# Attention and conformer kernel on one core: the sink logit as a column of the softmax, an early output projection taken apart, and a first stage in another order

## The chip, the cores and the metric

One core of one Trainium2 chip runs the whole kernel. The metric is device time in microseconds of one execution; the time before is 1807.06 us, the median of three runs (1806.05, 1807.06, 1809.84). One more execution was profiled: it took 1802.25 us.

## The reference, cut to what matters

Two layers on a stream of 1024 latent tokens of width 1024, with 256 context tokens. Layer 0 is windowed attention: 16 query heads of width 128, 4 key/value heads, a window of 128 tokens to each side, the 256 context keys in the same softmax, and one learned sink logit per head. Layer 1 is a conformer convolution module. The parts that the change touches:

```python
def sink_softmax(sink_l, *parts):
    sink_col = jnp.broadcast_to(sink_l..., first.shape[:-1] + (1,))
    p = jax.nn.softmax(jnp.concatenate([sink_col, *parts], axis=-1), axis=-1)
    ...                      # the sink's own column is dropped

for i in range(DEPTH):
    shift, scale, gate = jnp.split((silu_c @ ada_w[i] + ada_b[i])[:, None, :], 3, axis=-1)
    h_lat = modulate(rmsnorm(x, norm_g[i]), shift, scale)
    ...
    # attention: q, k, v, z = h_lat @ w_in; rope on q, k; y = (o * silu(z)) @ w_out
    x = x + gate * y
return rmsnorm(x, final_g)
```

So the sink takes part in the row's maximum and in the row's sum, and gives no output of its own.

## The kernel before, in words

Every large product is computed as three: each float32 operand is split into a high part (a copy rounded to the matmul's input type, `hi`) and a low part (`lo = full - hi`), and TensorE adds hi·hi, hi·lo and lo·hi. So each weight chunk and each activation tile costs a copy (mostly on ScalarE, ACT) and a subtraction (`split_lo`, on VectorE, DVE, or GpSimd, POOL) before TensorE (PE) may use it. In the profile these are `whi`/`wlo` for input weights (128x1024), `hh`/`hl` for the normalised tokens, `ahi`/`alo` for the modulation weights, `woh`/`wol` for the output weights, `ozh`/`ozl` for the gated attention output, `pthi`/`ptlo` for the transposed probabilities, `qh`/`ql`, `kh`/`kl`, `vh`/`vl` for queries, keys and values.

**First stage (0 to about 130 us).** Four row tiles `xs0` of 128 tokens are loaded, their sums of squares go to `sums`, `rstd_of` makes the factor `r` of a row in seven small operations on 128x4 elements (ACT's square root `sq`, DVE's `rr`, three `rq` and `r`), `normalise` scales the rows (two on DVE, two on ACT), PE turns them (`turn`, transposes by `ident`), `x_tile` applies the modulation and splits, `x_mm` multiplies by the chunks of k, q, v of head group 0. Before PE can do that, chunk 0 of the weights is split by `wsA.split(G)`: both halves on POOL. Then the second half of the tokens (`xs1`) follows in the same way, with `normalise(xs1, ...)` in the loop over `pr`. The rotary position of k and q (`finish`, lines 811 to 834) is a chain of a multiplication by `cos` (DVE), one by `sin` (POOL), a sum (DVE), a copy (ACT, `kh`/`qh`) and a subtraction (POOL, `kl`/`ql`); its last three steps are put off as one closure, `last`, in a deque `ropes0`, and one is popped per pass of the loop over `kt` at lines 1044 to 1060.

**Attention (130 to 860 us).** 16 heads times 8 query blocks. For each block `scores` (line 934) issues six matmuls into PSUM, a DVE reduction that adds the mask, writes `p` and gives the row maximum `mx`; a 128x1 operation on DVE that turns `mx` and the sink into `nmx` = min(-SCALE·mx, -sink); an exponential of the block on ACT with `nmx` as bias and the row sum `l0` as by-product; a second exponential of the sink alone, 128x1 (`es`); a 128x1 sum `l0 + es` and a reciprocal `ri` on DVE; and POOL scales `p` by `ri`. `fill(12)` then gives PE twelve matmuls of the next head's projections, `transposes` turns the scaled `p`, ACT copies the result (`pthi`) and DVE takes the difference (`ptlo`), and `pv` multiplies by v after every fourth block. In the background DVE builds the modulation of layer 1 (`mask_page`, scalar_tensor_tensor), takes low parts of the output weights (`low_parts`, `low_page`; a scheduling edge `after(..., anchor_max)` puts each behind the `nmx` of the last block), ACT makes `whi` and POOL `wlo` of the next weight chunk.

**Output projection of the attention (`proj_attn`, lines 645 to 735).** A generator. For each row pair `i` it loads `wo`, `wol` and (for the first column half) `ozf` (SyncE's queue, SP), splits them (`woh`, `ozh` on ACT, `ozl` on DVE) and multiplies. `EARLY_ROWS = 6` rows of it run in head 15 as filler matmuls: at step (15, 4) (line 1085, `EARLY_FROM = 4`) all of `lows` is run out and `EA + 1 = 3` steps of `projA` are taken. From 905 us on the rest of it, the conv layer and its output follow.

**What sets the order.** PE's order is the program's throughout. In the first stage DVE and ACT (`pin("PVA")`, later `pin("PV")`) are in program order too; from the attention on a list scheduler sets the order of ACT, DVE, POOL and SP at build time, and each engine then works its list strictly in order. So an instruction that waits holds back all that stands behind it on its engine. Tiles live in a pool of 45 pages (`pg`); `p` of a block and `wraw` of a weight chunk are such pages, so a first write to a page can also wait for the last reader of what lay in it before. In the trace all helper calls have line 88; so groups are told apart by tile names.

Of the kernel before, what the change touches and what calls it, by code (L numbers as in the profile page):

```python
# [12 lines left out]
ALU = mybir.AluOpType  # L13

P = 128
# [78 lines left out]
def backbone_kernel(  # L94
# [105 lines left out]
    class WStream:  # L200
# [19 lines left out]
        def split(self, hi_eng=None):  # L220
# [53 lines left out]
    wsA = WStream(chunks, nraw=4, lo_eng=lambda i: V if i in (2, 3) else G)  # L274
# [66 lines left out]
    def normalise(ts, ss, engs):  # L341
        r = rstd_of(ss, D, len(ts))
        for i, eng in enumerate(engs):
            if eng is A:
                act(ts[i], ts[i], AF.Copy, scale=r[:, i:i + 1])
            else:
                eng.tensor_scalar(out=ts[i], in0=ts[i], scalar1=r[:, i:i + 1], scalar2=1.0, op0=ALU.mult, op1=ALU.mult)

# [127 lines left out]
    normalise(xs0, ss0, (V, V, A, A))  # L476
    wsA.split(G)
# [13 lines left out]
    for pr in range(NPR):  # L491
# [4 lines left out]
        if pr + 2 < NPR:  # L496
            ada_split(pr + 2, (0, 1))
        x_mm(a, 0, acc0, which)
# [11 lines left out]
        if pr == 2:  # L510
            normalise(xs1, ss1, (G, G, A, G))
# [124 lines left out]
    def proj_attn():  # L636
# [64 lines left out]
        for i, (s, kk) in enumerate(seqB):  # L701
# [112 lines left out]
    def rope(o, sl, dh, dl, ropes=None):  # L814
# [16 lines left out]
        if ropes is None:  # L831
            last()
        else:
            ropes.append(last)
# [99 lines left out]
    def scores(h, qb):  # L934
# [14 lines left out]
        sc8 = small([P, 5], name="sc", bufs=6)  # L949
        mx, nmx, l0, es, ri = (sc8[:, i:i + 1] for i in range(5))  # L950
        w = nw + CT
        sc = dict(scale=1.0, scalar=-3.0e38, op0=ALU.add, op1=ALU.max, accum_out=mx)
        if qb == TB - 1:
            V.tensor_tensor_reduce(
# [4 lines left out]
        else:  # L959
            V.tensor_tensor_reduce(out=p[:, 0:w], in0=s[:, w0:768], in1=mask[:, 640 - w:640], **sc)  # L960
# [82 lines left out]
    for kt in range(KT):  # L1043
# [3 lines left out]
        if kt > 0 and ropes0:  # L1047
            ropes0.popleft()()
# [640 lines left out]
```

## Time and profile before

| | |
|---|---|
| runs shown | 1806.05, 1807.06, 1809.84 us; median 1807.06 |
| profiled execution | 1802.25 us; its span from first to last instruction 1800.5 us |
| mean granted TensorE clock | 0.988 |
| PE busy | 1725.7 us |
| DVE, ACT, POOL busy | 1247.2, 890.2, 787.9 us |
| instructions in the trace | 24003 |

The views are read as follows. A row of a timeline has start, duration, engine, operation and output <- inputs; in square brackets the idle time of the engine before it and what ended it. A row of the waits names the waiting engine and tile, who released it, the total, the count and the longest. A row of the windows has the length of a stretch, the busy time of each engine in it (count), the granted clock of TensorE as a share of full speed (PEclk), the DMA engines' busy share and GB/s. In the trace the DVE reduction of a block is CUSTOM_DVE_ANT_0 (or ANT_1) with a DVE_READ_ACCUMULATOR2_ANT behind it; in the order below both are "ISA".

### The profile page before, as it was taken

How to read it: one execution, taken by the hardware profiler on the slowest of the kernel's cores; microseconds unless marked ns; L12 is line 12 of the kernel's file. 1: busy time of each engine (PE TensorE's matmuls, PEld its weight loads, DVE VectorE, ACT ScalarE, POOL GpSimd, SP SyncE). 2: the span in 40 equal slices, each digit the busy share in tenths (PEclk: the TensorE clock that was granted, in tenths of full speed). 3: DMA queues.
4: the chain of work that ended last, by engine and by line, in shares of the span. 5: the costliest groups of instructions: out<-in, count | busy, mean ns of one | idle time of the engine just before them, and what ended most of it. 6: DMA issues, size and time to landing. Idle time of an engine off the chain costs nothing. (4 is left out here: it accounts for less than half of the span.)

```text
span 1800.5 us, 24003 instructions
## 1 busy us (share of the span) xinstructions
PE 1725.7 (96%) x8383; PEld 1419.1 (79%) x8383; DVE 1247.2 (69%) x2418; ACT 890.2 (49%) x1539; POOL 787.9 (44%) x614
## 2 busy tenths in 40 slices
PE   5989999999999999999899999999999999999997
PEld 2678888888887888788688887888888888788886
DVE  6766774776656774676513349999999999866823
ACT  6645553445434454444423436655656565366730
POOL 1243443333423344333100137998988789120300
PEclk8999999999999999999899999999999999999999
DMA  9224443444324443335676633111020202376981
GB/s 316 92 71 126 132 135 91 131 131 142 110 94 129 146 136 105 110 97 177 250 269 234 237 119 106 47 36 48 24 88 30 82 31 72 115 240 236 327 279 47
DMA packets 195327, 242.47 MB, mean 135 GB/s; under 512 B 11799, under 2 KB 126791, under 8 KB 195205
## 3 DMA queue, kind: packets, MB, share of 16 engines
q1 hardware_dynamic: 188516, 230.10, 38.8%
q10 hardware_dynamic: 6688, 10.83, 2.6%
q8 instruction: 66, 1.08, 0.2%
q14 instruction: 57, 0.46, 0.1%
HBM read 188.70 MB, written 41.69 MB: 128 GB/s over the span
## 5 line engine op out<-in xcount | busy, mean ns | idle before, releaser
L88 POOL TENSOR_TENSOR odd_half<-odd_half,prod_half 128x513 f32<-128x513 f32 (+2 forms) x252 | 318.1, 1269 | 21.0 <-ACT prod_half L88 7.5
L88 PE MATMUL psg<-hh_page,whi_page 128*128 128x512 f32 x600 | 238.3, 397 | 0.0
L88 PE MATMUL psg<-hh_page,wlo_page 128*128 128x512 f32 x600 | 237.3, 395 | 0.0
L88 PE MATMUL psg<-hl_page,whi_page 128*128 128x512 f32 x600 | 237.1, 395 | 0.0
L88 POOL TENSOR_SCALAR p_page<-p_page,sc 128x640 f32<-128x640 f32 (+1 forms) x128 | 104.5, 816 | 302.7 <-DVE sc L88 153.7
L88 POOL TENSOR_TENSOR wlo_page<-wraw_page,whi_page 128x1024 fp32r<-128x1024 f32 x72 | 175.3, 2436 | 122.6 <-ACT whi_page L88 88.9
L88 ACT ACTIVATE prod_half<-ubuf,dww 128x513 f32<-128x513 f32 (+2 forms) x252 | 165.0, 674 | 110.2 <-POOL odd_half L88 105.9
L88 PE MATMUL psg<-h2l_page,whi_page 128*128 128x512 f32 x456 | 179.3, 393 | 1.8 <-DVE h2l_page L88 1.8
L88 PE MATMUL psg<-h2h_page,whi_page 128*128 128x512 f32 x456 | 180.5, 396 | 0.0
L88 PE MATMUL psg<-h2h_page,wlo_page 128*128 128x512 f32 x456 | 179.5, 394 | 0.0
L88 ACT ACTIVATE p_page<-p_page,sc 128x640 f32<-128x640 f32 (+1 forms) x128 | 102.5, 801 | 142.7 <-DVE sc L88 135.6
L88 DVE SCALAR_TENSOR_TENSOR pss<-ubuf,wsum,pss 128x512 f32<-128x512 f32 (+3 forms) x270 | 172.6, 673 | 0.3
L88 DVE SCALAR_TENSOR_TENSOR pss<-ubuf,dww,pss 128x512 f32<-128x512 f32 (+3 forms) x270 | 172.4, 673 | 0.3
L88 PEld LDWEIGHTS psg<-hh_page,wlo_page 128*128 128x128 f32 x600 | 113.2, 189 | 26.6
L88 DVE TENSOR_TENSOR ptlo<-pss,pthi 128x640 fp32r<-128x640 f32 (+1 forms) x144 | 103.0, 716 | 41.8 <-ACT pthi L88 41.2
L88 PEld LDWEIGHTS psg<-hl_page,whi_page 128*128 128x128 f32 x600 | 113.4, 189 | 20.5
L88 PEld LDWEIGHTS psg<-hh_page,whi_page 128*128 128x128 f32 x600 | 113.3, 189 | 20.3
L88 ACT ACTIVATE pthi<-pss 128x640 fp32r<-128x640 f32 (+1 forms) x144 | 88.1, 612 | 83.1 <-PE pss L88 75.8
L88 ACT ACTIVATE whi_page<-wraw_page 128x1024 fp32r<-128x1024 f32 x87 | 91.6, 1054 | 69.1 <-PE psg L88 22.0
L88 PE MATMUL pso<-h2h_page,whi_page 128*128 128x512 f32 x312 | 122.9, 394 | 0.0
L88 PE MATMUL pso<-h2l_page,whi_page 128*128 128x512 f32 x312 | 122.8, 394 | 0.0
L88 PE MATMUL pso<-h2h_page,wlo_page 128*128 128x512 f32 x312 | 122.7, 393 | 0.0
(243 smaller groups left out, 4098.3 us busy)
## 6 DMA issues: line engine op xcount, KB each, us to landing
wraw_page<-in_conv_w_in_dram SPq DMA_DIRECT2D x48, 512.0 KB
wraw_page<-in_attn_w_in_dram SPq DMA_DIRECT2D x40, 512.0 KB
wo_page<-in_attn_w_out_dram SPq DMA_DIRECT2D x32, 512.0 KB
wol_page<-wolA SPq DMA_DIRECT2D x32, 512.0 KB
wo_page<-in_conv_w_out_dram SPq DMA_DIRECT2D x32, 512.0 KB
wol_page<-wolC SPq DMA_DIRECT2D x32, 512.0 KB
rope_half<-rope_half ACTq DMA_DIRECT2D x80, 128.0 KB
araw_page<-in_ada_w_dram SPq DMA_DIRECT2D x32, 256.0 KB
```

The lines of the kernel that those rows point to most:

```text
L88: r = f(*a, **k)
```

## The change

**Softmax.** `mx` and `es` go. The reduction multiplies by -SCALE itself, starts from the negative sink (`scalar=nsink`, a column of 128 values) and takes the minimum, so that its accumulator is `nmx`. ACT copies the negative sink into one more column `w` of `p` (128x1, from a constant), and one exponential over `w + 1` columns (641 or 513 in place of 640 or 512) gives `p` and the row sum with the sink in it. Per block, and there are 128, two 128x1 DVE operations and one 128x1 exponential go, one 128x1 copy on ACT comes. `low_parts` are now behind the reduction itself.

**Early output projection.** `run(lows)` and the first step of `projA` move from step (15, 4) to (15, 2), and one step each is taken at (15, 2), (15, 3), (15, 4). The last early row no longer splits the row after it. The loads of the residual rows `xr` are issued at `kk == 4` in place of 3.

**First stage.** The row factors `r` are computed before chunk 0 is split; its high part goes from POOL to ACT, its low part from POOL to DVE, and the scaling of the rows stands between the two. `normalise(xs1)` stands before `x_mm(a)` of `pr == 2` in place of behind it. The closure `last` becomes two, `add` and `low`; `low` is on DVE instead of POOL there, and pops begin at `kt > 2`.

```diff
-                if hi_eng:
-                    hi_eng.tensor_copy(h, r)
-                else:
-                    act(h, r, AF.Copy)
+                act(h, r, AF.Copy)
+                if between:
+                    between()
                 split_lo(self.lo_eng(i), l, r, h)
...
-    wsA = WStream(chunks, nraw=4, lo_eng=lambda i: V if i in (2, 3) else G)
+    wsA = WStream(chunks, nraw=4, lo_eng=lambda i: V if i in (0, 2, 3) else G)
...
-    normalise(xs0, ss0, (V, V, A, A))
-    wsA.split(G)
+    r0 = rstd_of(ss0, D, 4)
+    wsA.split(lambda: scale_rows(xs0, r0, (V, V, A, A)))
...
+        if pr == 2:
+            normalise(xs1, ss1, (G, G, A, G))
         x_mm(a, 0, acc0, which)
...
-            ahead(i, EA, 1)
+            ahead(i, EA, min(1, EARLY_ROWS - 1 - i))
...
-            if kk == 3:
+            if kk == 4:
...
-        def last():
+        def add():
             tt(V, r, r, w, ALU.add)
             act(dh, r, AF.Copy)
-            split_lo(G, dl, r, dh)
+
+        def low():
+            split_lo(G if ropes is None else V, dl, r, dh)
...
-        mx, nmx, l0, es, ri = (sc8[:, i:i + 1] for i in range(5))
+        nmx, l0, ri = (sc8[:, i:i + 1] for i in range(3))
         w = nw + CT
-        sc = dict(scale=1.0, scalar=-3.0e38, op0=ALU.add, op1=ALU.max, accum_out=mx)
+
+        act(p[:, w:w + 1], nsink[:, h:h + 1], AF.Copy)
+        sc = dict(scale=-SCALE, scalar=nsink[:, h:h + 1], op0=ALU.add, op1=ALU.min, accum_out=nmx)
...
-        anchor_max[:] = [V.tensor_scalar(out=nmx, in0=mx, scalar1=-SCALE, scalar2=nsink[:, h:h + 1], op0=ALU.mult, op1=ALU.min)]
-        act(p[:, 0:w], p[:, 0:w], AF.Exp, bias=nmx, scale=SCALE, accum_out=l0)
-        act(es, sink[:, h:h + 1], AF.Exp, bias=nmx)
-        tt(V, l0, l0, es, ALU.add)
+        anchor_max[:] = [least]
+        act(p[:, 0:w + 1], p[:, 0:w + 1], AF.Exp, bias=nmx, scale=-1.0, accum_out=l0)
         V.reciprocal(ri, l0)
...
-        if kt > 0 and ropes0:
+        if kt > 2 and ropes0:
             ropes0.popleft()()
...
+        if (h, qb) == (NH - 1, EARLY_FROM - 2):
+            run(lows)
+        if h == NH - 1 and EARLY_FROM - 2 <= qb < EARLY_FROM:
+            next(projA)
         if (h, qb) == (NH - 1, EARLY_FROM):
-            run(lows)
-            for _ in range(EA + 1):
-                next(projA)
+            next(projA)
             fillq.append((("wo", 0), early_proj()))
```

Three places show what stands where afterwards. The first is DVE's list in the first stage, from the last steps of the row factors (`rq`, `r`) to the first tiles of normalised tokens (`hf`, `hl`), before:

```order
L88 TENSOR_SCALAR rq_9_241<-rq_9_241 128x4
L88 TENSOR_TENSOR r_10_245<-rr_8_239,rq_9_241 128x4
L88 TENSOR_SCALAR x_page_97<-x_page_97,r_10_245 128x1024
L88 TENSOR_SCALAR x_page_98<-x_page_98,r_10_245 128x1024
L88 TENSOR_SCALAR hf_page_277<-psg_263,mod_176 128x512
L88 TENSOR_TENSOR hl_page_276<-hf_page_277,hh_page_275 128x512
```

and after:

```order
L88 TENSOR_SCALAR rq_9_241<-rq_9_241 128x4
L88 TENSOR_TENSOR r_10_245<-rr_8_239,rq_9_241 128x4
L88 TENSOR_SCALAR x_page_97<-x_page_97,r_10_245 128x1024
L88 TENSOR_SCALAR x_page_98<-x_page_98,r_10_245 128x1024
L88 TENSOR_TENSOR wlo_page_248<-wraw_page_105,whi_page_247 128x1024
L88 TENSOR_SCALAR hf_page_277<-psg_263,mod_176 128x512
L88 TENSOR_TENSOR hl_page_276<-hf_page_277,hh_page_275 128x512
```

One row has come, chunk 0's low part, behind the scaling; POOL's list loses both rows of chunk 0, and ACT's gets the high part ahead of its two rows `x_page`.

The second is DVE's list at the step from the last block of head 12 to the first of head 13: `sc_7062` is the small tile of the block (13, 0), the reductions are "ISA", and `rope_half` belongs to q of head 13. Before:

```order
L88 ISA p_page_7061,sc_7062<-pss_7054,mask_page_699 128x512
L88 ISA sc_7062 128x1
L88 TENSOR_TENSOR rope_half_7078<-psg_6962,cos_page_623 128x512
L88 TENSOR_TENSOR ptlo<-pss_7042,pthi 128x5x128
L88 SCALAR_TENSOR_TENSOR mask_page_699<-dww_raw,cs,mask_page_699 128x256
L88 TENSOR_SCALAR sc_7062<-sc_7062,nsink 128x1
L88 TENSOR_TENSOR low_page_7052<-low_page_7052,lhi_half_7110 128x512
L88 TENSOR_TENSOR sc_7062<-sc_7062 128x1
L88 RECIPROCAL sc_7062<-sc_7062 128x1
L88 TENSOR_TENSOR ptlo<-pss_7100,pthi 128x5x128
L88 SCALAR_TENSOR_TENSOR mask_page_699<-wsum_raw,cs,mask_page_699 128x256
L88 TENSOR_TENSOR rope_half_7078<-rope_half_7078,rope_half_7077 128x512
```

The same place after, where the small tile is `sc_6856` and the rope is `rope_half_6870`:

```order
L88 TENSOR_TENSOR rope_half_6870<-psg_6758,cos_page_623 128x512
L88 ISA p_page_6855,sc_6856<-pss_6848,mask_page_699,nsink 128x512
L88 ISA sc_6856 128x1
L88 TENSOR_TENSOR low_page_6846<-low_page_6846,lhi_half_6902 128x512
L88 TENSOR_TENSOR ptlo<-pss_6836,pthi 128x5x128
L88 SCALAR_TENSOR_TENSOR mask_page_699<-dww_raw,cs,mask_page_699 128x256
L88 RECIPROCAL sc_6856<-sc_6856 128x1
L88 TENSOR_TENSOR ptlo<-pss_6892,pthi 128x5x128
L88 SCALAR_TENSOR_TENSOR mask_page_699<-wsum_raw,cs,mask_page_699 128x256
L88 TENSOR_TENSOR rope_half_6870<-rope_half_6870,rope_half_6869 128x512
```

The small operation between the reduction and the exponential is gone, and with it the four rows that stood ahead of it; the low part has moved ahead of the first `ptlo`.

The third is ACT's list at the end of the last head, where `pthi` are copies of the last blocks' transposes and `woh`, `ozh` the splits of the output projection. Before:

```order
L88 ACTIVATE woh_page_8401<-wo_page_8364 128x1024
L88 ACTIVATE p_page_8275,sc_8276<-p_page_8275,sc_8276 128x640
L88 ACTIVATE sc_8276<-sink,sc_8276 128x1
L88 ACTIVATE pthi<-pss_8308 128x5x128
L88 ACTIVATE p_page_8323,sc_8324<-p_page_8323,sc_8324 128x512
L88 ACTIVATE sc_8324<-sink,sc_8324 128x1
L88 ACTIVATE woh_page_8622<-wo_page_8444 128x1024
L88 ACTIVATE pthi<-pss_8356 128x5x128
L88 ACTIVATE woh_page_8450<-wo_page_8395 128x1024
L88 ACTIVATE pthi<-pss_8388 128x4x128
L88 ACTIVATE ozh_page_8624<-ozf_page_8448 128x1024
```

After:

```order
L88 ACTIVATE p_page_8023,sc_8024<-p_page_8023,sc_8024 128x641
L88 ACTIVATE pthi<-pss_8054 128x5x128
L88 ACTIVATE woh_page_8332<-wo_page_8139 128x1024
L88 ACTIVATE ozh_page_8334<-ozf_page_8143 128x1024
L88 ACTIVATE p_page_8069,sc_8070<-p_page_8069,sc_8070 128x513
L88 ACTIVATE pthi<-pss_8100 128x5x128
L88 ACTIVATE pthi<-pss_8132 128x4x128
L88 ACTIVATE woh_page_8366<-wo_page_8188 128x1024
L88 ACTIVATE ozh_page_8368<-ozf_page_8192 128x1024
```

The two splits of output weights that stood ahead of the last two `pthi` are behind them or further ahead; none stands between the last exponential and the last `pthi`.

More of the change, by code (lines that the diff above doesn't have):

```diff
@@ L218, in load, with split @@
             self.nl += 1
-        def split(self, hi_eng=None):
+        def split(self, between=None):
             if self.ns >= self.nl:
@@ L339, in sums, with scale_rows @@
         return ss
-    def normalise(ts, ss, engs):
-        r = rstd_of(ss, D, len(ts))
+    def scale_rows(ts, r, engs):
         for i, eng in enumerate(engs):
@@ L347, in normalise @@
                 eng.tensor_scalar(out=ts[i], in0=ts[i], scalar1=r[:, i:i + 1], scalar2=1.0, op0=ALU.mult, op1=ALU.mult)
+    def normalise(ts, ss, engs):
+        scale_rows(ts, rstd_of(ss, D, len(ts)), engs)
     mods = [ctile([P, 4, 2], F32, f"mod{pr}") for pr in range(NPR)]
@@ L509, in backbone_kernel @@
             ssc = sums(cx, (A, A))
-        if pr == 2:
-            normalise(xs1, ss1, (G, G, A, G))
         if pr > 1:
@@ L831, in rope @@
         if ropes is None:
-            last()
+            add()
+            low()
         else:
-            ropes.append(last)
+            ropes.extend((add, low))
     vlate = {}
@@ L948, in scores @@
         p = pg.alloc(F32, [1024], "p")
-        sc8 = small([P, 5], name="sc", bufs=6)
-        mx, nmx, l0, es, ri = (sc8[:, i:i + 1] for i in range(5))
+        sc8 = small([P, 3], name="sc", bufs=6)
+        nmx, l0, ri = (sc8[:, i:i + 1] for i in range(3))
         w = nw + CT
-        sc = dict(scale=1.0, scalar=-3.0e38, op0=ALU.add, op1=ALU.max, accum_out=mx)
+        act(p[:, w:w + 1], nsink[:, h:h + 1], AF.Copy)
+        sc = dict(scale=-SCALE, scalar=nsink[:, h:h + 1], op0=ALU.add, op1=ALU.min, accum_out=nmx)
         if qb == TB - 1:
-            V.tensor_tensor_reduce(
+            least = V.tensor_tensor_reduce(
                 out=p[:, 0:w].rearrange("p (a b) -> p a b", a=2),
```

2 lines of the change are left out of this document (1 added, 1 removed).

## The prediction

> **What bounds the kernel now.** I read the page's busy times first, then the windows by stage, then the waits of TensorE (PE), then the timelines at its longest waits. The page:
>
> ```profile
> PE 1725.7 (96%) x8383; PEld 1419.1 (79%) x8383; DVE 1247.2 (69%) x2418; ACT 890.2 (49%) x1539; POOL 787.9 (44%) x614
> ```
>
> PE's matmuls are the same before and after, so all that can be won lies in the time in which PE stands, and in the stretches in which it works at a lower clock. The windows say in which stages those lie:
>
> ```profile
> 0.00:42.00 42.00, 21.92 (x74) 9.47 (x74) 25.80 (x36) 27.21 (x33) 6.98 (x10) 0.80 0.97 310
> 42.00:130.00 88.00, 77.48 (x410) 59.22 (x410) 61.02 (x109) 46.30 (x82) 30.48 (x22) 1.00 0.31 95
> 130.00:860.00 730.00, 706.21 (x3857) 602.14 (x3855) 483.02 (x1113) 342.57 (x724) 275.17 (x226) 1.00 0.41 125
> 860.00:905.00 45.00, 37.62 (x177) 31.91 (x177) 20.41 (x39) 19.46 (x31) 6.42 (x16) 0.89 0.67 242
> 905.00:1790.00 885.00, 882.25 (x3872) 716.40 (x3870) 651.20 (x1106) 453.57 (x669) 468.88 (x340) 1.00 0.40 132
> ```
>
> The second figure is PE's busy time. It stands 20.1 us up to 42, 10.5 to 130, 23.8 in the attention, 7.4 at its end, and 2.8 in the 885 us after it, 64.6 in all. That last row carries the argument: behind 905 us PE is the bound without a gap, so what is won ahead of it arrives at the end in full. The waits name who releases PE:
>
> ```profile
> PE pss L88 <- POOL p_page L88: 9.4, 14, 2.2
> PE psg L88 <- DVE x_page L88: 7.2, 2, 7.0
> PE pso L88 <- ACT pthi L88: 5.9, 3, 4.2
> PE pss L88 <- DVE sc L88: 5.8, 5, 3.2
> PE pso L88 <- DVE ptlo L88: 4.4, 6, 1.8
> PE psg L88 <- POOL x_page L88: 1.7, 2, 0.9
> ```
>
> The first, third and fourth row are the ends of the softmax chain, which the change shortens; the second and last are the row scaling of the first stage, which it rearranges. The `ptlo` row is not touched directly.
>
> **First stage: the start.** DVE, POOL and ACT around the row factors, and PE's wait behind them:
>
> ```profile
> 19.94 1.02 DVE L88 TENSOR_TENSOR rq<-rr 128x4 f32<-128x4 f32 x1
> 21.19 2.20 DVE L88 TENSOR_SCALAR rq<-rq 128x4 f32<-128x4 f32 x1
> 23.43 0.16 DVE L88 TENSOR_TENSOR r<-rr,rq 128x4 f32<-128x4 f32 x1
> 19.91 1.04 POOL L88 CAST whi_page<-wraw_page 128x1024 fp32r<-128x1024 f32 x1 [18.79 <-DMA wraw_page<-in_attn_w_in_dram]
> 21.03 2.34 POOL L88 TENSOR_TENSOR wlo_page<-wraw_page,whi_page 128x1024 fp32r<-128x1024 f32 x1
> 23.68 2.19 ACT L88 ACTIVATE x_page<-x_page,r 128x1024 f32<-128x1024 f32 x2 [3.99 <-DVE r L88]
> 24.43 0.47 PE L88 MATMUL psg<-ident,x_page 128*128 128x128 f32 x1 [7.05 <-DVE x_page L88]
> ```
>
> Two operations on four columns take 1.02 and 2.20 us where the last step on as many, `r`, takes 0.16, and they end at 20.96 and 23.39, with POOL's at 20.95 and 23.37: they wait POOL's work out. With chunk 0 off POOL they take about 0.16 each, which puts `r` at about 20.7 in place of 23.59. What is late next is ACT: the high part of chunk 0 (1.04 on POOL; taken as the same) from 19.9 to 20.97, then the two scalings of 2.19 to 23.2 in place of 25.87. So all behind it comes 2.3 to 2.7 us earlier; I take 2.3. The low part on DVE hides behind PE's transposes. Bounds: nothing, if the weights and modulation rows (DMA share 0.97 there) are not there sooner; 2.9 by `r` alone.
>
> **First stage: the rest.** Two waits of PE and the DVE rows ahead of them:
>
> ```profile
> 88.87 1.75 DVE L88 TENSOR_TENSOR rope_page<-rope_page,rope_half 128x512 f32<-128x512 f32 x1
> 91.28 0.66 PE L88 MATMUL pso<-ident,x_page 128*128 128x128 f32 x4 [2.19 <-DVE vl_page L88]
> 113.24 2.91 DVE L88 TENSOR_TENSOR rope_half<-rope_half,rope_half 128x512 f32<-128x512 f32 x1
> 116.07 0.15 DVE L88 RECIPROCAL sc<-sc 128x1 f32<-128x1 f32 x1
> 118.01 0.66 PE L88 MATMUL pss<-ident,p_page 128*128 128x128 f32 x4 [2.21 <-POOL p_page L88]
> ```
>
> At 91.28 PE waits for `vl`, which stands behind a rope sum of 1.75; that sum is now popped later, so `vl` starts up to 1.75 sooner: 1.7. The second low part that DVE takes over falls where PE has work, and costs nothing while it stays behind `vl`; ahead of it, it would give back about 0.7. At 118.01 the first block's reciprocal stands behind a rope sum of 2.91; in the new order it stands ahead, so the 2.21 go: 2.2. The moved `normalise(xs1)` takes the two waits for POOL's `x_page` (1.7), but puts a 1.1 us scaling on ACT ahead of a tile that PE wants: 0.8 net. Sum of the first stage: 2.3 + 1.7 + 2.2 + 0.8 = 7.0, with 3.5 to 9 as bounds (without the start and half the rest; with all of it).
>
> **Attention.** Per block there go, by the groups:
>
> ```profile
> L88 DVE TENSOR_SCALAR sc<-sc,nsink 128x1 f32<-128x1 f32 x128 | 26.5, 207 | 0.9
> L88 DVE TENSOR_TENSOR sc<-sc 128x1 f32<-128x1 f32 x128 | 30.4, 238 | 70.9 <-ACT sc L88 70.5
> L88 ACT ACTIVATE sc<-sink,sc 128x1 f32<-128x1 f32 x128 | 35.8, 280 | 0.0
> ```
>
> On DVE that is 57 us, on ACT 36 less a copy of 128x1, which the trace does not show: it lies between nothing and the 0.28 of the small exponential; 0.2 by a guess nearer to the upper end. None of this is PE's time. What counts is that the chain from the reduction to the scaled `p` is shorter by 0.21 + 0.28 + 0.24 = 0.73 us, and more where one of them stood in a queue. That a reduction with a column as first value, or 641 columns in place of 640, is dearer, no row shows; I take nothing, at most 0.1 per block, which is hidden likewise. The waits on this chain outside the two places treated apart: `p_page` 9.4 - 2.2 = 7.2 in 13, `sc` 5.8 - 3.2 = 2.6 in 4, so 9.8 us in 17, 0.58 each. A cut of 0.73 takes the short ones whole and leaves about 0.6 of each longer one: I take 6 of the 9.8. One more place is worth its own sum:
>
> ```profile
> 743.95 2.39 POOL L88 TENSOR_TENSOR wlo_page<-wraw_page,whi_page 128x1024 fp32r<-128x1024 f32 x1 [0.72 <-ACT whi_page L88]
> 744.65 1.98 DVE L88 SCALAR_TENSOR_TENSOR mask_page<-dww_raw,cs,mask_page 128x256 f32<-128x256 f32 x1
> 746.55 0.20 DVE L88 TENSOR_SCALAR sc<-sc,nsink 128x1 f32<-128x1 f32 x1
> 746.78 0.73 ACT L88 ACTIVATE p_page<-p_page,sc 128x512 f32<-128x512 f32 x1 [2.91 <-DVE sc L88]
> 751.07 0.39 PE L88 MATMUL pss<-kh_page,qh_page 128*128 128x256 f32 x1 [2.41 <-ACT qh_page L88]
> 752.00:758.60 6.60, 6.17 (x17) 4.91 (x18) 2.88 (x7) 2.27 (x5) 3.59 (x4) 0.50 0.31 106
> ```
>
> The exponential waits 2.91 us for a 0.2 us operation that stands behind a modulation step stretched by POOL; the copies and the rope sum stand behind the exponential, and PE stands 2.41 us. The last row shows the clock at 0.50 for 6.6 us afterwards: half of it, 3.3, is lost. In the new order the exponential can go at once, about 2.5 us sooner, and the rope sum comes 1 to 1.8 us sooner, since the low part and two `ptlo` still stand ahead of it. I take 1.6 + 3.3 = 4.9. The `ptlo` waits (4.4) I leave as they are; for new waits in the changed order of ACT, DVE and POOL I take off 1. Sum: 6 + 4.9 - 1 = 9.9, say 10; bounds 0 (below) and 17 (all of the 9.8, the place whole, and half the `ptlo` waits, 9.8 + 4.9 + 2.2).
>
> The Trainium skill, page "TensorE: Matmul & The Clock Gate", section "Part 1: The HAM clock gate", has the clock fall after an idle window of about 3.4 us; this trace differs, since 2.41 us were enough at 751.07, while 2.19 and 2.21 were not. By the page's rule the 3.3 would not be owed to this wait.
>
> **End of the attention.** The two longest waits after the start, and what stood ahead:
>
> ```profile
> 860.92 1.58 DVE L88 TENSOR_TENSOR ozl_page<-ozf_page,ozh_page 128x1024 fp32r<-128x1024 f32 x1 [0.45 <-ACT ozh_page L88]
> 864.32 0.96 PE L88 MATMUL pss<-ident,p_page 128*128 128x128 f32 x4 [3.22 <-DVE sc L88]
> 864.40:868.00 3.60, 3.60 (x14) 3.40 (x15) 3.44 (x7) 2.63 (x5) 0.00 (x0) 0.53 1.04 396
> 885.13 0.60 PE L88 MATMUL pss<-ident,p_page 128*128 128x128 f32 x4
> 889.53 1.06 ACT L88 ACTIVATE woh_page<-wo_page 128x1024 fp32r<-128x1024 f32 x1 [7.72 <-DMA wo_page<-in_attn_w_out_dram]
> 892.67 0.79 PE L88 MATMUL pso<-pthi,kvc_page 128*128 128x512 f32 x1 [4.16 <-ACT pthi L88]
> 892.60:898.60 6.00, 5.93 (x18) 5.01 (x19) 0.69 (x1) 1.07 (x2) 0.00 (x0) 0.50 0.61 218
> ```
>
> At 892.67 PE waits 4.16 us for a copy that stands on ACT behind a weight split which waited 7.72 us for its transfer; then it runs 6.0 us at 0.50, which costs 3.0. In the new order that split is behind the last copies: 7.2 go, and nothing else is late there: PE had transposed the last block by 885.73, a copy and a low part behind it (about 0.7 each) end by 887.2, and PE's other work lasts to 888.5. At 864.32 the reduction stands behind a low part of 1.58 us; with the loads begun two blocks earlier, one such split fewer stands there: 1.9 of the 3.22, and the 3.6 us at 0.53 (1.7). That is 3.6, less certain, so I count 2.8 of it. Sum: 10. Bounds: 4 (the early loads push other transfers of SP's queue late, and one of the two waits returns) and 12.
>
> **The sum.** 7.0 + 10 + 10 = 27 us. Against the profiled execution: 1802.25 - 27 = 1775.25. That execution was 4.81 us below the median of the runs; on the median it is 1807.06 - 27 = **1780.1 us**. The later `xr` loads fall where PE runs without a gap, and are counted at nothing.
>
> **The rivals.**
>
> *The attention only moves its waits.* Each of them is a collision of DVE's background work, stretched by POOL's `wlo` as at 744.65, with a due tile; the collisions stay, the lists are new, and 10 becomes 0. Then 17 us remain: 1790.1. For it: the `ptlo` waits have nothing to do with the chain. Against: the 0.73 is taken from every block.
>
> *The clock dips are not owed to the waits.* If 752 and 864 fall anyway, 3.3 and 1.7 stay: 1785.1. This is the page's rule taken at its word; the trace has each dip directly behind a wait, which speaks against it.
>
> *Transfers set the pace at both ends.* With a DMA share of 0.97 before 42 us and 1.04 at 864, the earlier work only waits for bytes, and the attention gives nothing: about 3 us, 1804. Against: PE's long waits are released by DVE and ACT, and only one transfer is named.
>
> *Slower: the sink copies block ACT.* The copy into column `w` is the first write to `p`'s page, and the scheduler puts it blocks ahead of its exponential; where it waits for POOL to leave the page, exponential and `pthi` behind it on ACT wait too, up to one `wlo`, 2.4 us each time. With the attention's gain gone this way (17 left), it decides from nine such events on (9 x 2.4 = 21.6, over 17 + 3.6); at twelve the time is 1790.1 + 28.8 = 1818.9. For it: ACT is in order, and such a place is seen at 889.53. Against: ACT works 342.57 of 730 us there, and pages come free blocks ahead.
>
> *More than forecast.* Every term at its upper bound: 9 + 17 + 12 = 38 us, 1769.1.
>
> **How the numbers follow.** Forecast 0.53, attention unmoved 0.22, clock 0.07, more 0.06, transfers 0.05, slower 0.07. A measurement can tell 0.2%, 3.6 us. Faster: 0.53 + 0.22 + 0.07 + 0.06 = 0.88; the same 0.05; slower 0.07. The range takes in forecast, clock and the unmoved attention with some of its bounds, 1769 to 1797; what is left out is transfers, slower, and the outer part of the rest.
>
> **What would show it.** Right: `rq` at 0.2 us each and PE's first transposes before 22.5; no 0.50 clock behind the last `pthi`; `p_page` and `sc` waits together under 7 us where they were 15.2; PE's idle time in the attention near 16. Wrong: PE's busy time changed, DVE releases of `ptlo` grown by what the chain lost, or ACT rows of 128x1 on `p_page` with idle time ahead of them.

## The result, and the profile after

The changed kernel takes 1781.78 us, the median of four runs (1780.23 to 1783.41), where the kernel before took 1806.55 (four runs, 1803.8 to 1809.84): a ratio of 0.9862 with a 95% interval of 0.9843 to 0.9881, 24.8 us less. The prediction was 1780.1, from 1769 to 1797. The profiled execution of the changed kernel took 1782.36 us, 19.9 less than the one of before (1802.25), so the two profiled executions lie closer together than the medians do.

PE's order is the same in both kernels, so the count of matmuls begun by a moment is a clock of its own: the windows from 0 to a moment give that count, and the moment at which the other kernel has begun as many. By 130, 860 and 905 us the kernel before had begun 482, 4338 and 4513; the changed one gets there at 121.6, 843.4 and 881.8. So 8.4 us are won in the first stage, 8.2 in the attention, 6.6 at its end, 23.2 in all; about 3 of them are lost again in what follows. The page of the changed kernel, and its windows cut at those places (columns as before: length, busy time of PE, weight loads, DVE, ACT and POOL, granted clock, DMA share, GB/s):

```profile
PE 1722.9 (97%) x8383; PEld 1419.1 (80%) x8383; DVE 1203.3 (68%) x2165; ACT 885.6 (50%) x1540; POOL 780.4 (44%) x610
```

```profile
121.60:843.40 721.80, 703.13 (x3858) 601.18 (x3856) 446.81 (x873) 334.82 (x716) 274.71 (x226) 1.00 0.42 126
843.40:882.00 38.60, 36.13 (x178) 30.76 (x178) 17.87 (x29) 19.32 (x30) 6.48 (x16) 0.91 0.70 256
882.00:1769.00 887.00, 883.67 (x3868) 717.48 (x3867) 650.78 (x1105) 454.22 (x668) 468.05 (x340) 1.00 0.41 134
```

In the attention PE stands 18.7 us where it stood 23.8; at its end 2.5 where it stood 7.4; behind it there is as little idle time as before. DVE's busy time fell by 44 us, and that alone is not the result: a kernel below whose DVE works 13 us more is as fast. The waits of PE (who waits, who releases, total, times, longest):

```profile
PE pss L88 <- DVE sc L88: 5.7, 5, 2.0
PE pss L88 <- DVE ptlo L88: 5.6, 8, 1.1
PE psg L88 <- DVE x_page L88: 4.6, 2, 4.4
...
PE pso L88 <- DVE ptlo L88: 3.5, 7, 1.1
...
PE pss L88 <- POOL p_page L88: 1.5, 4, 0.5
PE pss L88 <- ACT qh_page L88: 1.3, 1, 1.3
...
PE pso L88 <- ACT pthi L88: 0.4, 1, 0.4
```

The waits for the scaled block (`p_page`) went from 9.4 to 1.5 us, those for `pthi` from 5.9 to 0.4, the one for `qh` from 2.4 to 1.3. The waits for `ptlo` grew, from 4.4 and 2.7 to 3.5 and 5.6. Now the start, in DVE's, ACT's and PE's timelines:

```profile
20.15 0.16 DVE L88 TENSOR_TENSOR rq<-rr 128x4 f32<-128x4 f32 x1
20.35 0.17 DVE L88 TENSOR_TENSOR rq<-rq,ms 128x4 f32<-128x4 f32 x1
20.55 0.17 DVE L88 TENSOR_SCALAR rq<-rq 128x4 f32<-128x4 f32 x1
20.75 0.16 DVE L88 TENSOR_TENSOR r<-rr,rq 128x4 f32<-128x4 f32 x1
```

```profile
20.08 1.06 ACT L88 ACTIVATE whi_page<-wraw_page 128x1024 fp32r<-128x1024 f32 x1 [0.18 <-DMA wraw_page<-in_attn_w_in_dram]
21.05 2.17 ACT L88 ACTIVATE x_page<-x_page,r 128x1024 f32<-128x1024 f32 x2
```

```profile
21.76 0.47 PE L88 MATMUL psg<-ident,x_page 128*128 128x128 f32 x1 [4.38 <-DVE x_page L88]
```

The three `rq` take 0.5 us together where two of them alone took 3.2; `r` is there at 20.91 in place of 23.59, ACT's scalings end at 23.22 in place of 25.87, and PE begins 2.67 us sooner. At the first block of head 13, DVE, ACT and PE:

```profile
730.59 0.75 DVE L88 CUSTOM_DVE_ANT_1 p_page<-pss,mask_page,nsink 128x512 f32<-128x512 f32 x1
...
731.27 0.69 DVE L88 TENSOR_TENSOR low_page<-low_page,lhi_half 128x512 f32<-128x512 f32 x1
731.87 0.82 DVE L88 TENSOR_TENSOR ptlo<-pss,pthi 128x640 fp32r<-128x640 f32 x1
732.60 1.89 DVE L88 SCALAR_TENSOR_TENSOR mask_page<-dww_raw,cs,mask_page 128x256 f32<-128x256 f32 x1
```

```profile
731.50 0.71 ACT L88 ACTIVATE p_page<-p_page,sc 128x513 f32<-128x513 f32 x1
```

```profile
737.83 0.39 PE L88 MATMUL pss<-kh_page,qh_page 128*128 128x256 f32 x1 [1.30 <-ACT qh_page L88]
```

The exponential starts with no wait of its own, ahead of the modulation step of 1.89 us that it stood behind before (in the list printed above, three tiles stood between the reduction's two rows and the small operation, not four); PE waits 1.30 in place of 2.41. At the end of the attention, PE and ACT:

```profile
846.53 1.30 PE L88 MATMUL pss<-ident,p_page 128*128 128x128 f32 x5 [2.00 <-DVE sc L88]
848.31 0.69 PE L88 MATMUL pss<-kh_page,qh_page 128*128 128x384 f32 x1 [0.48 <-DVE ptlo L88]
...
872.47 0.40 PE L88 MATMUL pso<-pthi,kvc_page 128*128 128x512 f32 x1
```

```profile
842.28 1.06 ACT L88 ACTIVATE ozh_page<-ozf_page 128x1024 fp32r<-128x1024 f32 x1 [2.80 <-DMA ozf_page<-ozd]
...
869.98 0.60 ACT L88 ACTIVATE pthi<-pss 128x512 fp32r<-128x512 f32 x1 [2.58 <-PE pss L88]
...
876.04 1.06 ACT L88 ACTIVATE woh_page<-wo_page 128x1024 fp32r<-128x1024 f32 x1 [5.47 <-PE pso L88]
```

The last `pthi` waits for PE, not PE for it, and the weight split comes six microseconds behind it; the row at 872.47 has no wait. The other wait, 3.22 us before, is still there with 2.00 + 0.48.

### The profile page after: what moved, and what is told of

It is laid out like the page before. It is cut to its first block, busy times and chain, and to the rows that moved or that the text cites. A ratio compares the mean times of both kernels' runs of the same rounds, so it can differ in the third digit from the quotient of the medians.

```text
span 1780.1 us, 23728 instructions
## 1 busy us (share of the span) xinstructions
PE 1722.9 (97%) x8383; PEld 1419.1 (80%) x8383; DVE 1203.3 (68%) x2165; ACT 885.6 (50%) x1540; POOL 780.4 (44%) x610
## 3 DMA queue, kind: packets, MB, share of 16 engines
q8 instruction: 66, 1.08, 0.3%
## 5 line engine op out<-in xcount | busy, mean ns | idle before, releaser
L88 ACT ACTIVATE p_page<-p_page,sc 128x641 f32<-128x641 f32 (+1 forms) x128 | 102.9, 804 | 91.8 <-DVE sc L88 87.3
```

Source lines behind the costliest of these rows:

```text
L88: r = f(*a, **k)
```

## The experiments

All ratios are to the kernel before on the same chip, with 95% intervals; positions and waits are those of each profile.

**One part alone.** The softmax edit alone is the part of the diff under "mx, es"; the first stage's edit alone and the early projection's alone are the rest of it, as printed above.

> The kernel before with the softmax edit alone (sink as a column and as the minimum's first value). Theory (three separate gains): about 8 us come in the attention between 130 and 860 us, 4 of them at the first block of head 13, and about 2 at the first block of all; at the end of the attention the list still has a late weight split ahead of the last of the two pthi, so a wait of 3 us or more and a clock at 0.50 stay there: 10 us less than before in all (7 to 13), a ratio of 0.9945. Rival (the gains are not separate; only the three edits together make the new lists good): under 4 us.

Measured: 1792.44 us, ratio 0.9934 (0.9922 to 0.9946), 12 us less, in the range expected. Its `p_page` waits are 2.3 us, and PE waits 2.14 for `pthi` at the end, where 3 or more was expected. Between the 482nd and the 4338th matmul it wins 5.8 us in its profile, in place of the 8 expected.

> The kernel before with the first stage's edit alone. Theory: PE's first transposes at 21.8 in place of 24.4, the wait for vl at 0.5 in place of 2.2; 6 to 8 us less at the 10th block, and the attention and its end as before (waits of 2.4 us at head 13's first block, 3.2 and 4.2 at the end): 6.5 us less in all, a ratio of 0.9964. Rival (transfers set the pace of the start): of the 2.7 us nothing is left at 60 us and the whole gain is under 4.

Measured: 1796.43 us, ratio 0.9955 (0.9938 to 0.9972), 8 us less. PE's first transposes are at 20.45, of the start's gain 2.8 us are left at 60, and 8.7 are won by the 482nd matmul; from there to the end it keeps between 7.3 and 9.7. The rival, transfers, falls.

> The kernel before with the early projection's edit alone. Theory: the late split is behind the last two pthi, the wait of 4.2 us and the 6 us at 0.50 behind it go (7 us); the wait of 3.2 us ahead of it stays, as it did in the changed kernel: 7 us less in all (5 to 9), a ratio of 0.9961. Rival (it is the shorter softmax chain that emptied ACT's list there): under 3 us.

Measured: 1798.42 us, ratio 0.9964 (0.9951 to 0.9976), 6 us less. Up to 840 us it is as the kernel before to about 3 us; the wait for `pthi` is gone. The wait of 3.22 became two, 1.75 for `sc` and 1.04 for `ptlo`.

The three ratios multiply to 0.9853, which the ratio of the whole change, 0.9862, meets within its interval: three gains that add up, as far as intervals of about 2 us each can tell.

**Without the early edit.** The changed kernel, less these lines:

```diff
-        if (h, qb) == (NH - 1, EARLY_FROM - 2):
-            run(lows)
-        if h == NH - 1 and EARLY_FROM - 2 <= qb < EARLY_FROM:
-            next(projA)
         if (h, qb) == (NH - 1, EARLY_FROM):
-            next(projA)
+            run(lows)
+            for _ in range(EA + 1):
+                next(projA)
...
-            ahead(i, EA, min(1, EARLY_ROWS - 1 - i))
+            ahead(i, EA, 1)
...
-            if kk == 4:
+            if kk == 3:
```

> The changed kernel with the early projection's edit undone (softmax and first stage alone). Theory: 16 us ahead at 860 as in the changed kernel, then a wait of 3 us or more for the last pthi with a clock at 0.50 behind it: 15 to 18 us less than before in all, a ratio of 0.991. Rival (the early edit did nothing for PE): as fast as the changed kernel, 0.9862.

Measured: 1787.31 us, ratio 0.9905 (0.9893 to 0.9918), as expected. ACT and PE in its profile:

```profile
876.21 1.06 ACT L88 ACTIVATE woh_page<-wo_page 128x1024 fp32r<-128x1024 f32 x1 [8.03 <-DMA wo_page<-in_attn_w_out_dram]
877.17 0.58 ACT L88 ACTIVATE pthi<-pss 128x512 fp32r<-128x512 f32 x1
```

```profile
877.80 0.80 PE L88 MATMUL pso<-pthi,kvc_page 128*128 128x512 f32 x1 [5.35 <-ACT pthi L88]
```

This is the place of before again: a split that waits for its transfer stands ahead of a copy that PE waits for. Then the one line alone, put back into this kernel:

```diff
-            ahead(i, EA, 1)
+            ahead(i, EA, min(1, EARLY_ROWS - 1 - i))
```

> Softmax and first stage as changed, and of the early projection's edit only one line: the last early row does not split the row after it. Theory (that line moves the late weight split behind the last pthi): the wait of 5.4 us for pthi and the dip behind it are gone against the kernel without the early edit, a wait of about 4.4 us for sc about 30 us ahead of it stays, since the loads are not begun sooner; 21 us less than before, a ratio of 0.988. Rival (it is the spread of the loads that counts): as without the early edit, 0.9905.

Measured: 1778.52 us, ratio 0.9867 (0.9854 to 0.9881); no wait for `pthi` at all, and 4.5 for `sc` about 30 us ahead of the end. The one line is the whole of the early edit as far as the intervals can tell, some 2.5 us to each side: the kernel is as fast as with the loads spread. I had expected a ratio of 0.988, so about 3 us for the spread; but 4.5 is also what the changed kernel loses there in a second execution (below).

**The two halves of the softmax edit.** In one, the sink's exponential and sum are back; in the other, the maximum and the operation that makes the bias from it:

```diff
-        act(p[:, w:w + 1], nsink[:, h:h + 1], AF.Copy)
...
-        act(p[:, 0:w + 1], p[:, 0:w + 1], AF.Exp, bias=nmx, scale=-1.0, accum_out=l0)
+        act(p[:, 0:w], p[:, 0:w], AF.Exp, bias=nmx, scale=-1.0, accum_out=l0)
+        act(es, sink[:, h:h + 1], AF.Exp, bias=nmx)
+        tt(V, l0, l0, es, ALU.add)
```

> The changed kernel with only half of the softmax edit: the reduction still gives the negative maximum itself, but the sink has its own exponential of 128x1 and its sum again. Theory (it counts that nothing stands between the reduction and the exponential): the first block of head 13 stays at a wait of about 1.3 us, waits for p_page and sc grow by about 3 us in all, 21 to 22 us less than before, a ratio of 0.988. Rival (what counts is the shorter way from the exponential to the scaled block): the attention's gain of 8 is gone, a ratio of 0.991.

Measured: 1787.0 us, ratio 0.9909 (0.9895 to 0.9923), the rival's figure.

```diff
+        act(p[:, w:w + 1], sink[:, h:h + 1], AF.Copy, scale=1.0 / SCALE)
+        sc = dict(scale=1.0, scalar=-3.0e38, op0=ALU.add, op1=ALU.max, accum_out=mx)
...
+        anchor_max[:] = [V.tensor_scalar(out=nmx, in0=mx, scalar1=-SCALE, scalar2=nsink[:, h:h + 1], op0=ALU.mult, op1=ALU.min)]
+        act(p[:, 0:w + 1], p[:, 0:w + 1], AF.Exp, bias=nmx, scale=SCALE, accum_out=l0)
```

> The changed kernel with the other half alone: the sink as a column of one exponential, the maximum as before, with the 128x1 operation that makes the bias from it. Theory: the wait of 2.4 us at the first block of head 13 is back with a dip of the clock behind it, sc waits grow; 5 us slower than the changed kernel, a ratio of 0.989. Rival (the column is the half that counts): as fast as the changed kernel, 0.9862.

Measured: 1780.28 us, ratio 0.9879 (0.9865 to 0.9893), as fast as the changed kernel on the same scale, though PE waits 5.77 us for `p_page` about 30 us ahead of the attention's end, where the changed kernel waits 2.5 (4.5 in a second execution). My theory falls in both. The column carries the edit: from the 482nd to the 4234th matmul (130 to 840 us in the kernel before, 710.0 us) it takes 701.0 us, the other half 707.7, the whole edit 702.4. At the first block of head 13 each half takes a part of the wait, here with the column alone and then with the bias alone:

```profile
736.34 0.39 PE L88 MATMUL pss<-kh_page,qh_page 128*128 128x256 f32 x1 [1.92 <-ACT qh_page L88]
```

```profile
741.85 0.39 PE L88 MATMUL pss<-kh_page,qh_page 128*128 128x256 f32 x1 [1.83 <-ACT qh_page L88]
```

From 2.41, the one takes 0.49 and the other 0.58, together 1.07; both at once took 1.11. So both ends of the chain act at that place, though the cut is smaller than the 1.6 taken. The kernel with the bias alone has more waits for `ptlo` than the one with the column alone, 10.1 us in place of 7.3. The scheduling edge of the low parts hangs on the operation that makes the bias; with that operation gone it hangs on the reduction, and the low part moves up directly behind it. That was the next thing to try.

**The low parts behind `ptlo`.**

```diff
-                after(split_lo(V, raw[:, b], raw[:, b], hi[:, 0:512]), anchor_max)
+                after(split_lo(V, raw[:, b], raw[:, b], hi[:, 0:512]))
```

> The changed kernel with one argument altered: the scheduling edge of the low parts of the output weights hangs on the last ptlo in place of the last reduction. Theory (the ptlo waits, 9.1 us in 15, are a low part stretched by POOL to about 2 us that stands between a reduction and the ptlo behind it): these waits fall to 4 us or less, and the attention gains 4 us: 0.2% less than the changed kernel, a ratio of 0.9845. Rival (the low part only meets the next due tile there, a reduction, and PE waits for sc instead): within 1 us of the changed kernel.

Measured: 1770.39 us, ratio 0.9815 (0.9801 to 0.983), against 1780.51 and 0.987 (0.9856 to 0.9885) of the changed kernel on the same chip: 10 us less, more than twice what was expected, and the intervals do not touch. By the 4513th matmul it is at 872.8 us where the changed kernel's execution beside it is at 880.0, so 7.2 us are won before the output projection, all of it ahead of the 4234th matmul; about 1.5 more are a dip of the clock that did not come (last section). What the edge removes is seen in the changed kernel at one of the `ptlo` waits; DVE, POOL and PE:

```profile
315.80 1.80 DVE L88 TENSOR_TENSOR low_page<-low_page,lhi_half 128x512 f32<-128x512 f32 x1
317.53 0.67 DVE L88 SCALAR_TENSOR_TENSOR zs_page<-zs_page,psg 128x512 f32<-128x512 f32 x1
318.13 0.81 DVE L88 TENSOR_TENSOR ptlo<-pss,pthi 128x640 fp32r<-128x640 f32 x1
```

```profile
314.63 2.43 POOL L88 TENSOR_TENSOR wlo_page<-wraw_page,whi_page 128x1024 fp32r<-128x1024 f32 x1
```

```profile
318.99 0.50 PE L88 MATMUL pso<-ptlo,kvc_page 128*128 128x512 f32 x1 [1.14 <-DVE ptlo L88]
```

The low part lasts until 317.60, half a microsecond past POOL's operation, and `ptlo` is due behind it. At the same block with the edge moved:

```profile
315.43 0.82 DVE L88 TENSOR_TENSOR ptlo<-pss,pthi 128x640 fp32r<-128x640 f32 x1
316.17 0.48 DVE L88 SCALAR_TENSOR_TENSOR mask_page<-wsum_raw,cs,mask_page 128x256 f32<-128x256 f32 x1
316.56 0.69 DVE L88 TENSOR_TENSOR low_page<-low_page,lhi_half 128x512 f32<-128x512 f32 x1
```

and its waits for `ptlo` in the whole execution:

```profile
PE pss L88 <- DVE ptlo L88: 1.0, 1, 1.0
PE pso L88 <- DVE ptlo L88: 0.4, 2, 0.2
```

9.1 us became 1.4. Low parts that run beside a `wlo` for more than half a microsecond number 6 in the kernel before, 11 in the changed one (1.91 us each on average, in place of 0.69 with POOL idle) and 1 here. The rival is right in part: the waits for `sc` grew from 5.7 to 8.7, one of 2.77 among them behind a low part of 1.75 that now stands ahead of a reduction, and the wait for `qh` at head 13 is 2.25 in place of 1.30; the clock dips for 3.41 us behind each of these two. Over all, PE's idle time between the 482nd and the 4234th matmul fell from 18.5 us (17.8 in the second execution) to 13.0, while the stretch itself got shorter by more, 694.2 in place of 702.4 and 701.7. Taken from start to start of the same matmuls, against the changed kernel's 702.4, the first scores matmul behind the transposes comes 5.2 us sooner in sum and the product with `ptlo` 4.1, of which 2.5 and 3.0 show as idle time. So the rest of the gain lies at the same two places, in delays that the profile, whose matmul ends are modelled, does not show as idle. This is the fastest kernel of the study.

**The wait that stayed, 30 us ahead of the end.** Two scheduling edges in the changed kernel, so that the split of early row 3 comes behind the exponential and the reduction it stood ahead of:

```diff
-                act(oh, f, AF.Copy)
-                split_lo(V, ol, f, oh)
+                hi, lo = act(oh, f, AF.Copy), split_lo(V, ol, f, oh)
+                if i == 3:
+                    after(hi, [mark["exp", 3]])
+                    after(lo, [mark["least", 4]])
```

> The changed kernel with two scheduling edges: the split of one early row (its high part on ACT, its low part on DVE) stands behind the exponential of the block (15, 3) and behind the reduction of (15, 4), in place of ahead of them. Theory (PE's 2.0 us wait there is that reduction standing behind the low part): the wait falls to 0.9 or less, and if the dip of the clock behind it is owed to it, 3.4 us more come back: 4 us faster than the changed kernel, a ratio of 0.984. Rival (PE waits for the transfers there): the wait stays or moves behind, a ratio of 0.9862.

Measured: 1781.13 us, ratio 0.9879 (0.9866 to 0.9891), so the theory falls. The wait for `sc` fell to 1.08, and 2.77 for `ptlo` came 3.5 us later: it moved. Then the bytes:

```diff
-            SY.dma_start(out=wl.bitcast(F32), in_=wolA[m, kk])
+            if 1 <= i < EARLY_ROWS:
+                G.memset(wl.bitcast(F32), 0.0)
+            else:
+                SY.dma_start(out=wl.bitcast(F32), in_=wolA[m, kk])
```

> The changed kernel without the load of the weights' low parts for the early rows 1 to 5 (they are zeroed on POOL instead, so this kernel leaves out those rows' products with the low parts of the output weights): 2.5 MB less in the last steps of the attention. Theory (from the last experiment: the 4 us or so that PE stands 30 us ahead of the attention's end are transfers, with a DMA share of 1.04 from 840 to 856): the share falls under 1 there, and the waits of 2.0 and 0.5 and the dip behind them fall to under 1 us together; 2 to 5 us less than the changed kernel. Rival (it is the order on DVE): the 2.0 us stay.

Measured: 1781.03 us, ratio 0.9876 (0.9861 to 0.9891). The DMA share fell to 0.96 and 1.00 between 840 and 848 (1.04 in the changed kernel), hardly under 1, and the wait for `sc` is 3.81: this theory falls too. And the loads sooner:

```diff
-        if (h, qb) == (NH - 1, EARLY_FROM - 2):
+        if (h, qb) == (NH - 1, EARLY_FROM - 3):
             run(lows)
-        if h == NH - 1 and EARLY_FROM - 2 <= qb < EARLY_FROM:
+        if h == NH - 1 and EARLY_FROM - 3 <= qb < EARLY_FROM - 1:
             next(projA)
```

with the third step at `EARLY_FROM - 1`.

> The changed kernel with the early projection's first loads one block sooner, at (15, 1) to (15, 3). Theory (transfers): some of the bytes move ahead of 836 us and the wait of 2.0 us falls under 1; 1 to 4 us less than the changed kernel. Rival (SP's queue waits for free pages, so that what is issued sooner starts no sooner): the waits stay, within 1 us of the changed kernel.

Measured: 1780.54 us, ratio 0.987 (0.9851 to 0.9888); 1.61 for `sc` and 1.50 for `ptlo`. None of the three moves the time. The order of this one row's split is not the cause by itself, and neither is the moment of the first loads; of the transfers' mass the runs say less, since at 312 and 353 GB/s in place of 369 and 405 they stayed dense there. What the profiles of the changed kernel and of the kernel with fewer bytes share is the copy `ozh` on ACT that waits 2.80 and 2.35 us there for its `ozf`; why that transfer lands so late was not found, and stays open.

**The changed kernel again.**

> The changed kernel once more, unaltered, to see what of its profile belongs to one execution. Theory (a dip of the clock falls behind a given wait in some executions and not in others): PE's waits keep their places and lengths to 0.3 us, while the dip behind the 1.40 us wait 700 us ahead of the end, or the late warming of the clock at the start, is gone; the profiled spans differ by 1 to 3 us. Rival (a dip belongs to a wait): the same dips. A ratio of 0.987 to before in both cases.

Measured: 1780.51 us, ratio 0.987 (0.9856 to 0.9885). The two profiled spans are 1780.1 and 1777.8. The longer waits of the attention recur to 0.3 us (1.13, 1.07, 1.13, 1.29 and 1.10 where the first execution has 1.14, 1.00, 1.14, 1.30 and 1.10); the pair at the end does not, 1.93 + 2.57 in place of 2.00 + 0.48. The late warming of the clock at the start is gone, the late dip is there again; the last section shows both. Counted as above against the same profile of before, this execution is 10.2 us ahead at the 482nd matmul, 19.6 at the 4338th and 25.1 at the 4513th.

## Why the prediction was right, point by point

**What bounds the kernel.** Behind 905 us PE has no gap to swallow a gain, and the lead of 23.2 us at the 4513th matmul arrives at the end but for 3; of these a dip of the clock takes about 1.5, which no row of before could show; the rest was not traced to a place. The sum of 27 us compares with 24.8 by the medians and 19.9 by the profiled executions. That the forecast time, 1780.1, lies within 2 us of the measured 1781.78 is in part luck: the terms are off by +1.4, -1.8 and -3.4, and the pair of profiles shows 7 us less than the sum.

**First stage: 7.0 predicted, 8.4 measured, 10.2 in the second execution.** The start gave 2.7 in the rows where 2.3 was taken, and ACT was late next, as said; in this execution the clock then warmed two microseconds later and 1.4 was left at the 59th matmul, in the second execution 3.2. The wait for `vl` fell from 2.19 to 0.52 (1.7 taken), and the first block's wait of 2.21 is gone. The moved scaling took both waits for `x_page`, 2.0 us from start to start, and gave 1.4 back ahead of two other tiles: 0.6 where 0.8 was taken. About 2 more came from shorter waits for `hl` and in the blocks behind the first, which the sum did not hold. The rival that transfers set the pace there fell with the first stage alone, which kept 8 us.

**Attention: 10 predicted, 8.2 measured.** The waits on the chain, 9.8 us outside the two places, fell to 1.5 + 3.7 = 5.2, so 4.6 in place of 6. The place at head 13 gave 1.1 and the dip behind it 3.4, as against 1.6 and 3.3; that the dip went is in part luck, since the same wait of 1.3 us was followed by a dip in other kernels here (last section). The reserve of 1 for new waits was too small: `ptlo` grew by 2. The step that was off is the shares of the chain: 0.21 + 0.28 + 0.24 were taken as one cut of 0.73, wherever it falls. The halves show that the 0.28 and 0.24 behind the exponential carry it, and that the 0.21 ahead of it gained little. The likely reason is that with it the low parts lost the operation they were tied to and moved ahead of `ptlo`; the half with the bias was not run with its low parts moved, so this is argued. The order of DVE's list shown ahead of the prediction had that row moved up, and I counted it at nothing. The waits for `ptlo` grew by 2 us, and tying the low parts to `ptlo` wins 7 us in the attention of the changed kernel, more than it takes to undo the move.

**End: 10 predicted, 6.6 measured.** The larger wait is gone with its dip, 7.2 taken, and the weight split stands where the order had it. The smaller one, 2.8 taken, did not go: it cost 3.22 and 1.7 of the dip behind it, and now costs 2.00 + 0.48 and 3.4. The failed step is "with the loads begun two blocks earlier, one such split fewer stands there": the loads' place changes nothing that the runs can tell, as the one line alone shows.

**The rivals.** That the attention only moves its waits holds for `ptlo`, for 2 of 10 us. That the copies of the sink block ACT happens, and costs PE next to nothing. The group in the changed kernel (busy time, mean ns, idle time of ACT ahead of them and what ended it):

```profile
L88 ACT ACTIVATE p_page<-nsink 128x1 f32<-128x1 f32 x128 | 23.6, 195 | 31.4 <-DMA wolC<-low_page 12.9 <-DMA wolA<-low_page 10.3 <-PE psg L88 2.6
```

ACT stands 31.4 us ahead of the copies, 23.2 of it until a store of low parts has landed, so the sign named for this rival is there. Fifteen copies have more than 0.6 us ahead of them, up to 3.03. In the 4 us behind each, PE has a wait over 0.2 us after one alone, at head 13; there the next row on ACT, too, is a copy of a product of PE. So ACT had the room. The rival that the dips are not owed to the waits falls in its plain form; the last section says what they follow. The reduction with a column as first value is dearer by 0.06 us (859 ns in place of 798), within the 0.1 allowed.

**The signs.** The three `rq` took 0.17 us each and PE's first transposes began at 21.76, ahead of 22.5; no dip stands behind the last `pthi`. The waits for `p_page` and `sc` are 7.2 us where under 7 was said, and PE's idle time in the attention is 18.7 where 16 was said. Of the signs of being wrong, the waits for `ptlo` grew by 2 us, a part of what the chain lost.

## What to carry to other kernels

A background operation's scheduling edge is part of the critical chain's order: when an operation is removed that such an edge hangs on, look at where the background work moves to, and put the edge behind the operation that PE waits for next. An in-order engine that waits for a transfer holds up everything listed behind it, so look at each long wait for what stands ahead of the due instruction, not at its own cost. And read a gain off the count of matmuls at fixed places rather than off two end times; it separates what a stage won from what a dip of the clock took back.

## What the runs showed of the hardware

A dip of the granted clock to 0.50 does not follow from a wait's length alone. The same wait of 1.40 us for `h2l` 700 us ahead of the end stands in every kernel; the windows of 6 us over it, in the kernel before, in the changed one, in its second execution and in the one with the low parts moved (length, PE busy, granted clock, DMA share, GB/s):

```profile
1099.00:1105.00 6.00, 4.60 (x20) 1.00 0.33 91
```

```profile
1076.00:1082.00 6.00, 4.61 (x13) 0.72 0.33 97
```

```profile
1074.00:1080.00 6.00, 4.57 (x13) 0.72 0.31 87
```

```profile
1067.00:1073.00 6.00, 4.59 (x19) 1.00 0.34 93
```

PE is idle for 1.4 us in each, and in two of the four the clock falls, which takes 6 or 7 matmuls from the window. Likewise 1.92 us left the clock at 1.00 at head 13 with the column alone, and 1.30 let it fall in the kernel with the softmax alone.

The clock records of the fourteen traces show what it does follow. Each stretch at 0.50, but for the one behind PE's last matmul, starts on a grid of 3.41 us, fixed within an execution, and lasts a whole number of its steps. Between 45 and 1750 us the fourteen executions have 6953 such steps at full clock. All 24 with more than 1.81 us of PE idle time are followed by a dip, of the 16 between 1.60 and 1.81 eight are, and of the rest none. So about half a step of idle time, from one wait or several, lets the clock fall, and one wait that lies across two steps counts as two short ones. The wait of 1.40 us in the changed kernel, which lies in one step, and in the kernel before, where it lies across two, the steps of the grid as windows:

```profile
1074.96:1078.37 3.41, 1.71 (x5) 1.00 0.28 83
1078.37:1081.78 3.41, 3.41 (x9) 0.50 0.53 154
```

```profile
1096.56:1099.98 3.42, 2.24 (x8) 1.00 0.51 147
1099.98:1103.39 3.41, 2.81 (x12) 1.00 0.25 68
```

Where the grid lies against a wait differs from execution to execution. At head 13 a wait of 1.3 us stands in eight of the profiles, and a dip follows it in three; the wait of 2.41 us there, which a dip followed in the kernel before, had none behind it in the kernel with the early edit alone, where it lay across two steps with 1.77 and 1.26 us of idle time. The warming at the start moves in the same way; the windows of the changed kernel and of its second execution from 35 to 37 us:

```profile
35.00:37.00 2.00, 2.00 (x6) 0.50 1.05 337
```

```profile
35.00:37.00 2.00, 1.96 (x9) 1.00 1.08 342
```

The Trainium skill, page "TensorE: Matmul & The Clock Gate", section "Part 1: The HAM clock gate", says that the gate watches a free-running window of about 3.4 us; the grid of 3.41 us in these traces agrees with it. Its rule that an idle window of that length cools the clock understates it here: steps with 1.60 to 1.91 us of idle time were enough at waits of 1.30 and 1.40 us.

A subtraction of two operands in SBUF on DVE is stretched by POOL's subtraction (the low part, 0.69 us, took 1.80 under a `wlo` of 2.43), while `ptlo`, whose first operand is in PSUM, took 0.81 to 0.83 in the twelve cases of the changed kernel in which it ran beside a `wlo` for over half a microsecond, as it does with POOL idle. The Trainium skill, page "SBUF — State Buffer", section "Who interferes with whom", names two SBUF inputs as a condition for that, and the rows agree.
